# Third weight sums of the first two seven-product pairs ordered behind the operand's last low half, in a two-layer encoder trunk on one core

## The chip, the cores and the metric

The kernel runs on one core of one Trainium2 chip. The metric is the device time of one execution in microseconds (us), the median of several runs. A profiled execution gives the times of single instructions: PE is the matrix engine (TensorE), DVE is VectorE, ACT is ScalarE, POOL is GpSimd, and SP issues most transfers between the chip's main memory and its on-chip memory. Each engine works through a queue of its own in order; an instruction that waits holds up all that stand behind it on its engine, and nothing on the others unless they wait for it.

## The reference, cut to what matters

512 tokens of width 1024 go through two layers. In each, three token mixers (differential attention, a convolution module, neighbourhood attention) are merged by gates, projected and added to the residual stream; then come a gated feed-forward block of width 2816 and a gated input embedding:

```python
for i in range(DEPTH):                       # 2 layers
    ...
    merged = (ga * (ya @ w_br_a[i]) + gb * (yb @ w_br_b[i])
              + gc * (yc @ w_br_c[i]))
    x = x + merged @ w_o[i]
    h = rmsnorm(x, norm_ffn[i])
    x = x + (jax.nn.silu(h @ w_ffn_gate[i]) * (h @ w_ffn_up[i])) @ w_ffn_down[i]
    ...
```

The part that the change touches runs from the end of the merge, through `merged @ w_o` and the norm behind it, to the first blocks of the feed-forward products.

## The kernel before, in words

**Number format.** Matrix products are made in three passes. Every float32 operand is split into a high half (ScalarE, `act`, L143) and a low half (VectorE, the source minus the high half, `tt`, L157); `split` (L162) issues both. PE multiplies high by high, high by low and low by high (L177 to L179 in `mm3`, L983 to L985 in `seven`). So each weight and each activation that PE uses has been through ScalarE and then VectorE.

**The stages around the change.** `merge_b` (L767) ends the merge: its eight results are split into tiles that the profile calls mergeb_y and mergeb_v. `w_o` (L886) multiplies them by the output weights in eight groups of 24 matmuls (wo_mm), adds the residual (wo_x) and makes the operand for the next block (wo_h). The first two groups form a pair: PE does seven of eight chunks of each, and the last chunk of both at the end, so the last mergeb_v is needed there. The sum of squares goes through the norm (`norm`, L206): PE transposes it (L213), VectorE reduces it (L215) and scales it (L218), POOL takes the power (L222), PE transposes the result (L226).

**The feed-forward block** (`ffn`, L1039) runs over 22 blocks fb of 128 columns, in three parts of 8, 7 and 7. Block 0 multiplies gate and up weights by the operand in the plain way. Every other block is one pair of a gate and an up product in `seven` (L940), which replaces eight half-size products by seven. These need sums of weights and sums of the operand:

- The operand's sums are made by `quarters` (L911), once per pair of chunks. For j = 0 to 2 it is called from `w_o`, after chunks 2, 4 and 6, and for j = 3 from `ffn`, right ahead of block 0's products. Each call makes t1 to t4 on VectorE and splits them; for j = 2 and 3 the halves lie in wo_z tiles.
- The weights' sums are s1 = gate left + up left and s2 = up right + up left (both by a transfer that adds on arrival: SP loads at L950 and L951, POOL issues the accumulating transfers at L955), the third sum s3 = s1 + a22, and s4 = s3 + the right half of the gate weights. s3 and s4 are VectorE additions (L157, output ffn_qk, input ffn_r or ffn_wr). s1|s2, the gate weights, a22 and s3|s4 are then split. a22 is loaded at L953 (ffn_r), the gate weights at L952 (ffn_wr). The halves of s3|s4 are the tiles ffn_pt (odd fb) and ffn_y (even fb).

PE takes the products of a block in the order a11, a22, s2, a12, s1, s3, s4, so s3|s4 is wanted last.

**What sets the order.** PE's order is the order of the program text. The other engines are ordered by a scheduler that goes by priorities and by when inputs are estimated to be there; `seven` issues its loads and sums under a raised priority (L944), so they can stand far ahead of the stage they belong to. Where that is not wanted, `behind(i, then)` (L1020) gives instruction i a pure order behind `then`, without a semaphore. `seven` has three such orders. s3 stands behind the low half of a22 (L970). Where its argument `first` is true, for the first two blocks of the second and of the third part, s3 also stands behind `self.held` (L972), the low half that finished the block before. And the gating of the block before is ordered behind a copy (L1014).

Buffers: s3 and s4 have one buffer for all blocks; a22 has two (fb = 1, 2, then 3 takes that of 1); gate weights share three with all other weights.

Of the kernel before, what the change touches and what calls it, by code (L numbers as in the profile page):

```python
# [61 lines left out]
class Net:  # L62
# [848 lines left out]
    def quarters(self, x, h, j):  # L911


        one, two = slice(0, 256), slice(256, 512)
        g = lambda k: self.par(self.i, "ffn", k)
        f = []
        for k in (2 * j, 2 * j + 1):
            v = self.sb("t", [P, 512])
            self.act(v, x[k], AF.Copy, scale=g(k))
            f.append(v)  # L920
        b11, b12, b21, b22 = f[0][:, one], f[0][:, two], f[1][:, one], f[1][:, two]
        u = self.sb("t", [P, 2, 256])
        w = self.sb("t", [P, 2, 256])
        t1, t2, t3, t4 = u[:, 0], u[:, 1], w[:, 0], w[:, 1]
        self.tt(t1, b11, b12, ALU.subtract)
        self.tt(t2, b22, t1, ALU.add)
        self.tt(t3, b22, b12, ALU.subtract)
        self.tt(t4, t2, b21, ALU.subtract)
        if j < 2:
            d = [self.sb("rp" if n < 2 else "e", [P, 2, 256], F32R) for n in range(4)]  # L930
        else:
            d = [q for n in range(2) for q in self.zs[2 * j - 4 + n]]
        for o, t in zip(d, (t1, t2, t3, t4)):
            self.split(o[:, 0], o[:, 1], t)
        ha, hb = self.halves(h[2 * j]), self.halves(h[2 * j + 1])
        cut = lambda p, c: (p[0][:, c], p[1][:, c])
        return dict(b11=cut(ha, one), b21=cut(hb, one), b22=cut(hb, two),
                    **{f"t{n + 1}": (o[:, 0], o[:, 1]) for n, o in enumerate(d)})

    def seven(self, wg, wu, bs, tags, spare, md, first):  # L940


        nc = self.nc
        with self.tc.high_priority(offset=min(self.w_ahead, self.tc.cur_priority - self.p0)):  # L944
            lo, up = slice(0, 512), slice(512, 1024)
            g, a22 = self.sb("wr", [P, 1024]), self.sb("r", [P, 512])
            sums = self.sums[self.sevens % 3], self.sums[3]
            self.sevens += 1
            s1, s2, s3, s4 = (s[:, q:q + 512] for s in sums for q in (0, 512))
            nc.sync.dma_start(s1, wg[:, lo])  # L950
            nc.sync.dma_start(s2, wu[:, up])  # L951
            nc.sync.dma_start(g, wg)  # L952
            nc.sync.dma_start(a22, wu[:, up])  # L953
            for q in (s1, s2):
                nc.gpsimd.dma_start(q, wu[:, lo], accum_op=ALU.add)  # L955
            ws = {}

            def halve(hi, lo, src, names):
                i = self.split(hi, lo, src)
                for q, name in enumerate(names):  # L960
                    c = slice(q * 512, q * 512 + 512)
                    ws[name] = (hi[:, c], lo[:, c])
                return i

            wide = lambda: (self.sb("wh", [P, 1024], F32R), self.sb("wl", [P, 1024], F32R))
            halve(*wide(), g, ("a11", "a12"))
            low = halve(self.sb("kh", [P, 512], F32R), self.sb("a", [P, 512], F32R), a22, ("a22",))
            halve(*wide(), sums[0], ("s1", "s2"))
            i = self.tt(s3, s1, a22, ALU.add)
            self.behind(i, low)  # L970
            if first:
                self.behind(i, self.held)  # L972
            self.tt(s4, s3, g[:, up], ALU.add)
            halve(*spare, sums[1], ("s3", "s4"))
        A, C, Q = (self.ps(t, (P, 2, 256)) for t in tags)

        def product(out, w, b, first):
            wh, wl = ws[w]
            mm = nc.tensor.matmul
            for k in range(4):  # L980
                c = slice(k * P, k * P + P)
                bh, bl = bs[k][b]
                mm(out, wh[:, c], bh, start=first and k == 0, stop=False, skip_group_check=True)  # L983
                mm(out, wh[:, c], bl, start=False, stop=False, skip_group_check=True)  # L984
                mm(out, wl[:, c], bh, start=False, stop=k == 3, skip_group_check=True)  # L985
            self.chunk2()

        o = self.sb("t", [P, 2, 256])
        p1, p4 = o[:, 0], o[:, 1]
        p5 = self.sb("a", [P, 256])  # L990
        gg, uu = self.sb("t", [P, 2, 256]), self.sb("t", [P, 2, 256])
        product(A[:, 0], "a11", "b11", True)
        self.act(p1, A[:, 0], AF.Copy)
        product(Q[:, 0], "a22", "t4", True)
        self.act(p4, Q[:, 0], AF.Copy)
        product(C[:, 0], "s2", "t1", True)
        self.flush(self.act(p5, C[:, 0], AF.Copy))
        product(A[:, 0], "a12", "b21", False)
        product(Q[:, 0], "s1", "t3", False)
        product(A[:, 1], "s3", "t2", True)  # L1000
        product(C[:, 0], "s4", "b22", False)
        rb = self.rb.rearrange("p (a b) -> p a b", a=2)
        self.tt(p5, p4, p5, ALU.subtract)
        self.tt(gg[:, 0], A[:, 0], rb[:, 0], ALU.mult)
        self.tt(p1, A[:, 1], p1, ALU.subtract)
        self.tt(uu[:, 0], p1, Q[:, 0], ALU.subtract)
        self.tt(uu[:, 1], uu[:, 0], p5, ALU.add)
        self.tt(gg[:, 1], C[:, 0], p1, ALU.subtract)
        self.tt(gg[:, 1], gg[:, 1], rb[:, 1], ALU.mult)

        def rest(then):
            i = self.act(gg, gg, AF.Silu, table="silu")
            if then is not None:
                self.behind(i, then)  # L1014
            self.tt(gg, gg, uu, ALU.mult)
            self.held = self.split(md[:, 0, :], md[:, 1, :], gg.rearrange("p a b -> p (a b)"))

        self.pending.append(rest)
# [20 lines left out]
    def ffn(self, h, x):  # L1039
# [3 lines left out]
        st, hn, bs = [], [], self.four  # L1043
        spare = [[self.sb(t, [P, 1024], F32R) for _ in range(2)] for t in ("y", "pt")]
        md8 = [self.sb(t, [P, 2, 512], F32R) for t in ["v"] * 4 + ["z"] + ["y"] * 3]
        self.sums, self.sevens = [t for _ in range(2) for t in self.parts_of("qk", [1024], 2)], 0
        for part in PARTS:
            mids = []
            for f, fb in enumerate(part):
                tags = (("mm", "mm", "mm"), ("sc", "sc", "av"))[fb % 2]  # L1050
                md = md8[f]
                mids.append(md)
                wg, wu = self.a["w_fg"][i, fb], self.a["w_fu"][i, fb]
                if fb:
                    self.seven(wg, wu, bs, tags, spare[fb % 2], md, part[0] and f < 2)
                    continue
                g = self.sb("t", [P, 512])
                pg, pu = (self.ps(t) for t in tags[:2])
                for j in range(len(QUARTERS), 4):
                    self.four.append(self.quarters(x, h, j))  # L1060
                self.pair((pg, pu), (wg, wu), [h[k] for k in ORDER])

                def gate(pg=pg, g=g):
                    self.tt(g, pg, self.rb, ALU.mult)
                    self.act(g, g, AF.Silu, table="silu")

                self.ready(gate)

                def up(pu=pu, g=g, md=md):
                    self.tt(g, g, pu, ALU.mult)  # L1070
                    self.split(md[:, 0, :], md[:, 1, :], g)

                self.ready(up)
            self.flush()
            down = [self.a["w_fd"][i, m][:, part[0] * P:(part[-1] + 1) * P] for m in range(KD)]
            two = [self.ps(("mm", "sc")[fb % 2 == 0]) for _ in range(2)]
            self.pair(two, down[:2], mids)
            for m in range(KD):
                if m < 2:
                    ps = two[m]  # L1080
                else:
                    ps = self.ps("mm")
                    self.gemm(ps, down[m], mids)
                d = self.sb("t", [P, 512])
                self.tt(d, ps, self.rb, ALU.mult)
                self.tt(x[m], x[m], d, ALU.add)
                if part is PARTS[-1]:
                    if m in (0, 2):
                        qk = self.parts_of("qk", [2, 512], 2, F32R)
                    hn.append(self.norm_chunk(m, x[m], self.par(i, "ple", m),  # L1090
                                              qk[m % 2] if m < 4 else "z", st))
# [315 lines left out]
```

## Time and profile before

| what | value |
|---|---|
| median of three runs | 1793.07 us (1792.29 to 1793.09) |
| the profiled execution's own time | 1792.81 us |
| its span, from first to last instruction | 1791.0 us |
| PE, DVE, ACT busy in the span | 99%, 79%, 50% |
| mean granted clock of TensorE | 0.998 |

The page of the profile has the busy time of each engine, the chain of work that ended last, and groups of instructions. The timeline of an engine gives for each instruction its start and duration in us, its line, output and inputs, and in brackets how long the engine was idle ahead of it and what released it. Starts of neighbouring instructions can be closer than their durations, since instructions of one engine overlap a little. The granted clock (PEclk) is the share of full speed that TensorE's throttle allowed.

### The profile page before, as it was taken

To read this page: it belongs to the slowest core of one execution; us is meant where nothing else is said; L and a number is where in the kernel's file an instruction comes from. 1 tells how busy PE (TensorE), PEld (TensorE's weight loads), DVE (VectorE), ACT (ScalarE), POOL (GpSimd) and SP (SyncE) were. 2 spreads that over 40 slices of the span, in tenths; PEclk is the share of its full clock that TensorE was granted. 3 is DMA by queue.
4 is the path that set the end of the run, shared out by engine and by line. 5 is a ranking of instruction groups with operands and counts; after the bars stand their busy time and mean duration, and the time that the engine had idled before them with its cause. 6 is when DMAs were issued, how large, how long until landed. Compare 5 with 4: busy or idle time off the path is not lost.

```text
span 1791.0 us, 27255 instructions
## 1 busy us (share of the span) xinstructions
PE 1774.5 (99%) x10138; PEld 1559.7 (87%) x10138; DVE 1410.6 (79%) x2394; ACT 891.6 (50%) x1551; POOL 99.3 (6%) x142
## 2 busy tenths in 40 slices
PE   9999999999999999999999999999999999999998
PEld 7888888888799899998888888888887998989987
DVE  7877888997788587787776788889887885877776
ACT  5577555325565254454535765552355652534444
POOL 0000000000111011100000000000001110101000
PEclk9999999999999999999999999999999999999999
DMA  5665541334747365544447655422356563746332
GB/s 206 190 182 169 159 124 46 108 98 150 217 130 188 111 166 154 140 123 127 145 125 200 170 161 148 112 71 95 97 182 186 153 173 108 182 133 159 98 103 94
DMA packets 112212, 254.48 MB, mean 142 GB/s; under 512 B 14416, under 2 KB 19024, under 8 KB 112080
## 3 DMA queue, kind: packets, MB, share of 16 engines
q1 hardware_dynamic: 99264, 229.40, 41.9%
q0 software_dynamic: 12096, 22.03, 7.8%
q8 instruction: 80, 1.31, 0.3%
q10 hardware_dynamic: 720, 1.31, 0.2%
q14 instruction: 52, 0.43, 0.1%
HBM read 213.89 MB, written 7.34 MB: 124 GB/s over the span
## 4 chain that ended last, share of the span: by engine, by line
PE 91%; DVE 4%; DMA 2%; ACT 2%; issue 1%; SPq 0%; DVEq 0%; POOLq 0%; ACTq 0%
PE ffn_mm L177 5%; PE ffn_mm L178 5%; PE ffn_mm L179 5%; PE ffn_mm L985 4%; PE ffn_mm L984 4%; PE ffn_mm L983 4%; PE ffn_sc L985 3%; PE ffn_sc L984 3%; PE ffn_sc L983 3%; PE mergea_mm L178 2%; PE mergea_mm L179 2%; PE mergea_mm L177 2%; PE diff_sc L784 2%; PE gatec_mm L177 2%; PE gatec_mm L178 2%; PE gatec_mm L179 2%
## 5 line engine op out<-in xcount | busy, mean ns | idle before, releaser
L160 DVE SCALAR_TENSOR_TENSOR conv_z<-glu_z,pre_par,conv_z 128x512 f32<-128x512 f32 x240 | 179.6, 748 | 3.3
L143 ACT ACTIVATE ffn_wh<-ffn_wr 128x1024 fp32r<-128x1024 f32 (+1 forms) x94 | 94.9, 1015 | 110.0 <-PE ffn_mm L178 75.1
L157 DVE TENSOR_TENSOR ffn_wl<-ffn_wr,ffn_wh 128x1024 fp32r<-128x1024 f32 (+1 forms) x94 | 109.9, 1174 | 5.1 <-ACT ffn_wh L143 4.6
L955 POOL DMA_DIRECT2D ffn_qk<-w_fu x84 | 74.6, 996 | 550.5 <-DMA ffn_qk<-w_fu 218.1
L157 DVE TENSOR_TENSOR ffn_t<-ffn_mm,wo_rb 128x512 f32<-128x512 f32 (+1 forms) x66 | 40.0, 607 | 68.3 <-PE ffn_mm L179 68.3
L143 ACT ACTIVATE mergea_wh<-mergea_wr 128x1024 fp32r<-128x1024 f32 (+1 forms) x32 | 27.1, 846 | 96.8 <-PE mergea_mm L178 79.5
L177 PE MATMUL ffn_mm<-ffn_v,ffn_wh 128*128 128x512 f32 x176 | 68.5, 389 | 0.0
L178 PE MATMUL ffn_mm<-ffn_v,ffn_wh 128*128 128x512 f32 x176 | 68.5, 389 | 0.0
L179 PE MATMUL ffn_mm<-ffn_v,ffn_wl 128*128 128x512 f32 x176 | 68.5, 389 | 0.0
L157 DVE TENSOR_TENSOR ffn_wl<-ffn_qk,ffn_wh 128x1024 fp32r<-128x1024 f32 x42 | 51.4, 1225 | 19.9 <-ACT ffn_wh L143 19.9
L143 ACT ACTIVATE ffn_wh<-ffn_qk 128x1024 fp32r<-128x1024 f32 x42 | 44.5, 1060 | 43.7 <-PE ffn_mm L178 24.5
L157 DVE TENSOR_TENSOR ffn_t<-ffn_t,ffn_t 128x512 f32<-128x512 f32 (+1 forms) x48 | 31.4, 659 | 32.1 <-ACT ffn_t L143 31.5
L143 ACT ACTIVATE diff_a<-diff_sc,diff_s 128x512 f32<-128x512 f32 x32 | 22.0, 687 | 59.0 <-DVE diff_s L875 59.0
L983 PE MATMUL ffn_sc<-wo_h,ffn_wh 128*128 128x256 f32 x176 | 50.0, 284 | 0.0
L985 PE MATMUL ffn_sc<-wo_h,ffn_wl 128*128 128x256 f32 x176 | 49.8, 283 | 0.0
L984 PE MATMUL ffn_sc<-wo_h,ffn_wh 128*128 128x256 f32 x176 | 49.8, 283 | 0.0
L143 ACT ACTIVATE natten_wh<-natten_wr 128x1024 fp32r<-128x1024 f32 x24 | 25.4, 1058 | 41.4 <-issue 15.2
L984 PE MATMUL ffn_mm<-wo_h,ffn_wh 128*128 128x256 f32 x160 | 45.3, 283 | 0.0
L985 PE MATMUL ffn_mm<-wo_h,ffn_wl 128*128 128x256 f32 x160 | 45.3, 283 | 0.0
L983 PE MATMUL ffn_mm<-wo_h,ffn_wh 128*128 128x256 f32 x160 | 45.3, 283 | 0.0
L875 DVE TENSOR_REDUCE diff_s<-diff_sc 128x1 f32<-128x512 f32 x64 | 42.0, 684 | 3.5 <-PE diff_sc L784 3.4
L143 ACT ACTIVATE ffn_kh<-ffn_r 128x512 fp32r<-128x512 f32 x42 | 26.6, 632 | 32.8 <-PE ffn_mm L984 16.2
(825 smaller groups left out, 6577.0 us busy)
## 6 DMA issues: line engine op xcount, KB each, us to landing
ffn_wr<-w_fg SPq DMA_DIRECT2D x44, 512.0 KB, 3.9
ffn_qk<-w_fu POOLq DMA_DIRECT2D x84, 256.0 KB, 5.5
ffn_wr<-w_fd SPq DMA_DIRECT2D x32, 448.0 KB, 3.8
ffn_r<-w_fu SPq DMA_DIRECT2D x42, 256.0 KB, 4.8
ffn_qk<-w_fg SPq DMA_DIRECT2D x42, 256.0 KB, 3.9
ffn_qk<-w_fu SPq DMA_DIRECT2D x42, 256.0 KB, 4.2
natten_wr<-w_in SPq DMA_DIRECT2D x16, 512.0 KB, 4.1
natten_b<-bias SPq DMA_DIRECT2D x32, 256.0 KB, 3.8
```

Source lines behind the costliest of these rows:

```text
L143: i = self.nc.scalar.activation(out, in_, func, **kw)
L157: return self.nc.vector.tensor_tensor(out, a, b, op)
L160: return self.nc.vector.scalar_tensor_tensor(out, a, s, b, op0, op1)
L177: mm(out, wh, ah, start=first, stop=False)
L178: mm(out, wh, al, start=False, stop=False)
L179: mm(out, wl, ah, start=False, stop=last)
L784: self.nc.tensor.matmul(out, st4[:, u, qs], st[:, ks], start=n == 0, stop=n == 1)
L875: nc.vector.tensor_reduce(out=m[:, u:u + 1], in_=sc, op=ALU.max, axis=AX.X, negate=True)
L955: nc.gpsimd.dma_start(q, wu[:, lo], accum_op=ALU.add)
L983: mm(out, wh[:, c], bh, start=first and k == 0, stop=False, skip_group_check=True)
L984: mm(out, wh[:, c], bl, start=False, stop=False, skip_group_check=True)
L985: mm(out, wl[:, c], bh, start=False, stop=k == 3, skip_group_check=True)
```

## The change

`quarters` now keeps the last low half that it makes in `self.held`, and `seven` is told its block. For blocks 1 and 2, in each layer, s3 is ordered behind `self.held` as well. At that point `self.held` is the low half of t4 for j = 3: `quarters` is called for j = 3 ahead of block 0's products, and no block has yet set `self.held` anew when blocks 1 and 2 issue their sums. For the blocks that had the order already, nothing changes. The instructions and their operands stay the same; their places in the queues of VectorE, ScalarE and SP can change.

```diff
         for o, t in zip(d, (t1, t2, t3, t4)):
-            self.split(o[:, 0], o[:, 1], t)
+            self.held = self.split(o[:, 0], o[:, 1], t)
...
-    def seven(self, wg, wu, bs, tags, spare, md, first):
+    def seven(self, wg, wu, bs, tags, spare, md, first, fb):
...
             i = self.tt(s3, s1, a22, ALU.add)
             self.behind(i, low)
-            if first:
+            if first or fb < 3:
                 self.behind(i, self.held)
             self.tt(s4, s3, g[:, up], ALU.add)
...
-                    self.seven(wg, wu, bs, tags, spare[fb % 2], md, part[0] and f < 2)
+                    self.seven(wg, wu, bs, tags, spare[fb % 2], md, part[0] and f < 2, fb)
```

In the order that the scheduler then builds, in each layer: on VectorE s3 of block 1 moves from between two merge instructions to behind the last wo_z, s4 and the low half of s3|s4 to behind the norm's first instructions, two other pairs of neighbours change places; on ScalarE the high half of s3|s4 moves to behind the last wo_z; on SP the load of a22 for block 3 moves from ahead of three residual reads to behind the gate weights of block 3. PE and POOL keep their order.

## The prediction

> **What bounds the kernel now.** I read four views in this order: the page's busy shares with its chain, the waits of PE, the timelines of PE and VectorE around the longest of those waits, and the table of windows with the granted clock. From the page, the busy shares and the chain by engine:
>
> ```profile
> PE 1774.5 (99%) x10138; PEld 1559.7 (87%) x10138; DVE 1410.6 (79%) x2394; ACT 891.6 (50%) x1551; POOL 99.3 (6%) x142
> ...
> PE 91%; DVE 4%; DMA 2%; ACT 2%; issue 1%; SPq 0%; DVEq 0%; POOLq 0%; ACTq 0%
> ```
>
> PE is busy for 99% of the span and carries 91% of the chain that ended last. Work taken off any other engine is worth nothing by itself; only PE's idle or slowed time can be won. So the next view is the list of what PE waited for, the two longest entries (total, times, longest):
>
> ```profile
> PE wo_mm L178 <- DVE mergeb_v L157: 6.0, 2, 3.6
> PE pre_av L323 <- DVE pre_zeror L379: 1.1, 1, 1.1
> ```
>
> One wait stands out: 6.0 us in two pieces, one in each layer. In both, the output projection (wo_mm) waits for a low half that VectorE makes from the merged mixers (mergeb_v). All other entries are 1.1 us or less. PE's timeline at the first piece (start, duration, and in brackets the idle time before it and its releaser):
>
> ```profile
> 462.69 0.39 PE L177 MATMUL wo_mm<-mergeb_v,wo_wh 128*128 128x512 f32 x1
> ...
> 463.37 0.39 PE L177 MATMUL wo_mm<-mergeb_v,wo_wh 128*128 128x512 f32 x1
> 467.31 0.50 PE L178 MATMUL wo_mm<-mergeb_v,wo_wh 128*128 128x512 f32 x1 [3.56 <-DVE mergeb_v L157]
> ...
> 469.26 0.39 PE L177 MATMUL wo_mm<-mergeb_y,wo_wh 128*128 128x512 f32 x1
> ```
>
> and at the second:
>
> ```profile
> 1350.15 0.39 PE L177 MATMUL wo_mm<-mergeb_v,wo_wh 128*128 128x512 f32 x1
> 1352.99 0.75 PE L178 MATMUL wo_mm<-mergeb_v,wo_wh 128*128 128x512 f32 x1 [2.46 <-DVE mergeb_v L157]
> ...
> 1356.74 0.39 PE L178 MATMUL wo_mm<-mergeb_y,wo_wh 128*128 128x512 f32 x1
> ```
>
> The idle time is not the whole loss, so I count slips: how much later a matmul starts than it would at the undisturbed pace. The pace is three matmuls in 463.37 - 462.69 = 0.68 us, 0.227 us each. The matmul at 469.26 is the ninth after the one at 463.37; undisturbed it would start at 463.37 + 9 x 0.227 = 465.41. The first slip is 3.85 us. The matmul at 1356.74 is the tenth after 1350.15; undisturbed 1350.15 + 10 x 0.227 = 1352.42. The second slip is 4.32 us, although its wait was the shorter one. The table of windows says why (time, PE's busy time and count, then the other engines, PEclk, DMA share, GB/s):
>
> ```profile
> 467.30:469.30 2.00, 1.99 (x9) 1.65 (x10) 1.21 (x2) 1.40 (x2) 0.88 (x1) 1.00 0.88 182
> ...
> 1353.00:1356.50 3.50, 3.50 (x8) 2.76 (x9) 1.70 (x3) 2.44 (x3) 1.73 (x2) 0.51 1.09 233
> ```
>
> After the second wait the granted clock was 0.51 for 3.5 us, and eight matmuls took the time of some fifteen; after the first it was 1.00. What held VectorE in both places is seen in its own timeline, layer one and then layer two:
>
> ```profile
> 456.99 0.69 DVE L157 TENSOR_TENSOR gatec_x<-gatec_x,gateb_v 128x512 f32<-128x512 f32 x1
> 465.96 0.69 DVE L157 TENSOR_TENSOR ffn_qk<-ffn_qk,ffn_r 128x512 f32<-128x512 f32 x1 [8.29 <-DMA ffn_qk<-w_fu]
> 466.57 0.69 DVE L157 TENSOR_TENSOR mergeb_v<-gatec_x,mergeb_v 128x512 fp32r<-128x512 f32 x1
> ```
>
> ```profile
> 1351.64 0.69 DVE L157 TENSOR_TENSOR ffn_qk<-ffn_qk,ffn_r 128x512 f32<-128x512 f32 x1 [7.18 <-DMA ffn_qk<-w_fu]
> 1352.25 0.69 DVE L157 TENSOR_TENSOR mergeb_v<-gatec_x,mergeb_v 128x512 fp32r<-128x512 f32 x1
> ```
>
> The instruction that waits is s3 = s1 + a22 of fb = 1 (output ffn_qk), far ahead of its stage: it waits 8.29 and 7.18 us for the accumulating transfer into s1. The last low half of the merged operand stands right behind it in VectorE's queue, and PE waits for that one.
>
> **The change, part by part.** In each layer the added order puts s3 of fb = 1 behind the last low half of quarters (j = 3). s4, which adds to s3, the high half of s3|s4 on ScalarE and its low half on VectorE go with it. Nothing is added or removed in the arithmetic.
>
> (1) The wait in front of mergeb_v goes. What is late there next? VectorE is free when gatec_x ends, at 456.99 + 0.69 = 457.68, and its other input is the high half on ScalarE:
>
> ```profile
> 457.71 0.63 ACT L143 ACTIVATE mergeb_v<-gatec_x 128x512 fp32r<-128x512 f32 x1 [1.70 <-DVE gatec_x L157]
> ```
>
> It ends at 458.34, so the low half ends near 459.1. PE wants it one pace after 463.37, at 463.60: 4.5 us of margin. Both slips go whole: 3.85 + 4.32 = **8.17 us**.
>
> (2) What is moved costs VectorE 0.60 us for s3 (465.96 to the next start at 466.57), and in its old place for s4 and the low half, and ScalarE for the high half:
>
> ```profile
> 490.77 0.69 DVE L157 TENSOR_TENSOR ffn_qk<-ffn_qk,ffn_wr 128x512 f32<-128x512 f32 x1
> ...
> 492.85 1.22 DVE L157 TENSOR_TENSOR ffn_pt<-ffn_qk,ffn_pt 128x1024 fp32r<-128x1024 f32 x1
> ```
>
> ```profile
> 491.49 1.06 ACT L143 ACTIVATE ffn_pt<-ffn_qk 128x1024 fp32r<-128x1024 f32 x1
> ```
>
> That is 0.69 + 1.22 us of VectorE and 1.06 us of ScalarE that leave the stretch around 491 and land where VectorE and its neighbours look like this (VectorE; then POOL; then PE):
>
> ```profile
> 507.08 1.09 DVE L157 TENSOR_TENSOR wo_z<-ffn_t,wo_z 128x256 fp32r<-128x256 f32 x3
> 508.09 0.69 DVE L215 TENSOR_REDUCE wo_sm<-wo_tr 128x4 f32<-128x512 f32 x1
> 508.88 0.17 DVE L218 TENSOR_SCALAR wo_sm<-wo_sm 128x4 f32<-128x4 f32 x1
> 512.98 1.22 DVE L157 TENSOR_TENSOR ffn_wl<-ffn_qk,ffn_wh 128x1024 fp32r<-128x1024 f32 x1 [3.93 <-ACT ffn_wh L143]
> ```
>
> ```profile
> 509.13 1.03 POOL L222 TENSOR_TENSOR wo_rc<-wo_sm,pre_power 128x4 f32<-128x4 f32 x1 [38.93 <-DVE wo_sm L218]
> ```
>
> ```profile
> 512.59 0.60 PE L226 MATMUL wo_tr<-pre_ident,wo_rc 128*128 128x128 f32 x4
> 520.22 0.28 PE L983 MATMUL ffn_sc<-wo_rp,ffn_pt 128*128 128x256 f32 x1
> ```
>
> In the built order s3 stands behind the last wo_z and ahead of the reduction, s4 between the reduction and L218, the low half behind L218. So the chain reduction, L218, POOL, L226 gets 0.60 for s3 and as much for s4, 1.20 us, in front of it. POOL ends at 509.13 + 1.03 = 510.16, PE wants the column at 512.59: 2.43 us of margin, 1.23 left. The rest fits VectorE's hole of 3.93 us; the low half is needed by PE at 520.22, some 8 us after its new end. Cost 0; if the cover were gone, it could cost at most the 1.20 us per layer. From below it could even gain: VectorE loses up to 0.69 + 1.22 us of work ahead of the last wo_z and may get there earlier. But that is no time on PE; 0.
>
> (3) VectorE itself must follow PE. Up to the last wo_z it is nearly full:
>
> ```profile
> 495.00:508.00 13.00, 13.00 (x61) 10.78 (x60) 12.55 (x26) 10.73 (x20) 0.00 (x0) 1.00 0.33 110
> ```
>
> Its chain hangs on the ends of PE's wo_mm groups, which come earlier by the slip, and up to 1.91 us of work leave it. I take it to move with PE; that it stays where it is, is a rival below.
>
> (4) The transfer of a22 for fb = 3 needs the buffer that s3 reads. On SP it stood ahead of three reads of the residual; the built order puts it behind those and seven weight loads. The rows are its old issue, and ScalarE's high half of that a22:
>
> ```profile
> 466.68 0.33 SPq L953 DMA_DIRECT2D ffn_r<-w_fu  x1
> ```
>
> ```profile
> 526.06 0.63 ACT L143 ACTIVATE ffn_kh<-ffn_r 128x512 fp32r<-128x512 f32 x1 [0.94 <-PE ffn_mm L984]
> ```
>
> SP now stands behind it until s3 has read, about 508.09 + 0.60 = 508.7 on the old clock, and the transfer still has 17 us. Behind it on SP waits only the gate weight of fb = 4 and what follows, wanted later still. POOL's queue keeps its order: its accumulating transfers do not read s3. 0, with nothing at either end while the 17 us hold. The residual reads go out earlier, and only get margin.
>
> (5) For fb = 2 the added order changes nothing. Its s3 already stands behind the last wo_z:
>
> ```profile
> 518.29 0.69 DVE L157 TENSOR_TENSOR ffn_qk<-ffn_qk,ffn_r 128x512 f32<-128x512 f32 x1
> ```
>
> The sum: 8.17 us less, against the profiled execution 1792.81 - 8.17 = 1784.64 us. That execution lies 0.26 us below the median of the runs, so I forecast **1784.9 us** for the median.
>
> The unsure part of the sum is the clock. Beyond idle time the first slip has 3.85 - 3.56 = 0.29 us, the second 4.32 - 2.46 = 1.86 us, 1.57 more. If in the timed runs neither wait were followed by a slow stretch, the gain is 8.17 - 1.57 = 6.60; if both were, 9.74. I take the profiled row, since the three runs agree within 0.80 us, less than one such stretch.
>
> The Trainium skill, "TensorE: Matmul & The Clock Gate", Part 1, says that the clock halves after an idle window of about 3.4 us of a free-running counter. Here the row differs: the wait of 2.46 us was followed by 0.51, that of 3.56 us by 1.00. By that rule the slow stretch would not come from the second wait, and might not go with it; the sum would then be an estimated 6.6 us instead of 8.2.
>
> **The rivals.**
> - *The slow stretch stays.* The 0.51 has another cause, or comes in other runs differently. For it: the longer wait had none. Against: it begins at the very matmul that ends the wait. Gain 6.60, 1786.5 us; with both stretches in the runs before, 9.74, 1783.3 us.
> - *VectorE does not follow PE.* If the last wo_z stays at its absolute time, L226 stands 3.85 us earlier, and with 1.20 added against 2.43 of margin PE waits 2.62 us; in layer two, by the same margin, 4.32 + 1.20 - 2.43 = 3.09. Given back 5.71, gain 2.46: 1790.6 us. For it: the 12.55 of 13.00 us. Against: the moved work leaves exactly this stretch.
> - *The wait moves along with s3* (slower). s3 would wait at its new place as long as now, in front of the norm's reduction, and L226 would be late by 1.20 + 8.29 - 2.43 = 7.06 and 1.20 + 7.18 - 2.43 = 5.95 us: 13.01 - 8.17 = 4.84 us slower, 1797.9 us. It costs from a wait of 1.23 us on, and is slower than before from 1.23 + 8.17 / 2 = 5.3 us per layer. Against: s1 has landed by 465.96, some 38 us ahead of the new place.
> - *Nothing changes*: the low half of mergeb_v meets another wait as long. Then 1793.1 us. Against: part 1's 4.5 us of margin.
>
> **How the numbers follow.** Forecast 0.80, slow stretch 0.08, VectorE not following 0.05, wait moved 0.04, nothing 0.03. The range takes in the bounds of the clock, 1783.3 to 1786.5, with half the spread of the runs (0.40) below and the whole of it above, for a small part given back: 1782.9 to 1787.3 us; that holds the first two cases, and leaves the other 0.12 out. A difference of 0.2% (3.6 us) is about what a measurement of this kernel can tell from no change. Faster by more: 0.80 + 0.08 = 0.88. Within: 0.05 + 0.03 = 0.08. Slower: 0.04.
>
> **What would show it.** The waits of PE lose the entry on mergeb_v; the granted clock is 1.00 through the wo stage of both layers; s3 of fb = 1 appears behind the last wo_z without a wait; L226 has no idle time before it; ffn_wl behind the moved work starts as early, against PE, as now. If PE waits at L226, or for ffn_pt, the second rival holds in part; a slow stretch without a wait shows the first; s3 waiting for its transfer shows the third.

## The result, and the profile after

| | median, us | lowest to highest | runs |
|---|---|---|---|
| before | 1793.09 | 1792.29 to 1794.55 | 5 |
| after | 1784.92 | 1784.47 to 1785.96 | 5 |

The ratio after to before is 0.9953, with a 95% interval of 0.9939 to 0.9968: 8.2 us less. The profiled execution of after took 1785.96 us, its span is 1784.2 us.

The list of PE's waits in the profile after (engine and line, what it waited for, total us, times, longest):

```profile
PE natten_tr L709 <- ACT natten_e L143: 1.1, 2, 0.7
PE pre_av L323 <- DVE pre_zeror L379: 1.1, 1, 1.1
PE natten_tr L709 <- DVE natten_a L157: 0.9, 4, 0.3
PE diff_mm L588 <- ACT diff_rp L143: 0.6, 2, 0.3
PE natten_tr L709 <- DVE natten_pt L157: 0.6, 1, 0.6
```

The entry of 6.0 us on mergeb_v is gone, in both layers, and nothing of its size has come up. VectorE around the place that s3 has left (start, duration, line, output and inputs, idle time before it and its releaser):

```profile
457.58 0.68 DVE L157 TENSOR_TENSOR gatec_x<-gatec_x,gateb_v 128x512 f32<-128x512 f32 x1
458.97 0.69 DVE L157 TENSOR_TENSOR mergeb_v<-gatec_x,mergeb_v 128x512 fp32r<-128x512 f32 x1 [0.70 <-ACT mergeb_v L143]
464.84 1.37 DVE L157 TENSOR_TENSOR wo_x<-wo_x,wo_mm 128x512 f32<-128x512 f32 x2 [5.18 <-PE wo_mm L179]
```

The last low half of the merged operand now waits 0.70 us for its high half, and VectorE is then idle for 5.18 us until PE has finished: at this place VectorE waits for PE, no longer PE for VectorE. PE itself goes through the place at its pace, in the first layer:

```profile
463.96 0.39 PE L177 MATMUL wo_mm<-mergeb_v,wo_wh 128*128 128x512 f32 x1
464.18 0.39 PE L178 MATMUL wo_mm<-mergeb_v,wo_wh 128*128 128x512 f32 x1
```

The low half ended at 458.97 + 0.69 = 459.66, and PE read it at 464.18: 4.5 us of margin. Where s3 has gone to, on VectorE, then POOL, then PE:

```profile
503.40 1.09 DVE L157 TENSOR_TENSOR wo_z<-ffn_t,wo_z 128x256 fp32r<-128x256 f32 x3
504.40 0.69 DVE L157 TENSOR_TENSOR ffn_qk<-ffn_qk,ffn_r 128x512 f32<-128x512 f32 x1
505.01 0.69 DVE L215 TENSOR_REDUCE wo_sm<-wo_tr 128x4 f32<-128x512 f32 x1
505.61 0.69 DVE L157 TENSOR_TENSOR ffn_qk<-ffn_qk,ffn_wr 128x512 f32<-128x512 f32 x1
506.21 0.17 DVE L218 TENSOR_SCALAR wo_sm<-wo_sm 128x4 f32<-128x4 f32 x1
507.42 1.22 DVE L157 TENSOR_TENSOR ffn_pt<-ffn_qk,ffn_pt 128x1024 fp32r<-128x1024 f32 x1 [1.04 <-ACT ffn_pt L143]
```

```profile
506.46 1.03 POOL L222 TENSOR_TENSOR wo_rc<-wo_sm,pre_power 128x4 f32<-128x4 f32 x1 [35.73 <-DVE wo_sm L218]
```

```profile
509.33 0.60 PE L226 MATMUL wo_tr<-pre_ident,wo_rc 128*128 128x128 f32 x4
516.96 0.28 PE L983 MATMUL ffn_sc<-wo_rp,ffn_pt 128*128 128x256 f32 x1
```

s3 waits for nothing. POOL has the norm's column at 506.46 + 1.03 = 507.49, PE takes it at 509.33: 1.84 us of margin. The low half of s3|s4 ends at 508.64, 8.3 us before PE uses it. The granted clock in both wo stages is seen in this execution's table of windows (time, PE busy and count, the other engines, PEclk, DMA share, GB/s), the first layer's and the second's:

```profile
460.00:465.00 5.00, 5.00 (x24) 4.14 (x23) 0.16 (x1) 0.34 (x1) 1.02 (x2) 1.00 0.97 252
465.00:475.00 10.00, 10.00 (x46) 8.29 (x45) 9.22 (x14) 7.62 (x12) 2.65 (x3) 1.00 1.09 298
1345.00:1350.00 5.00, 5.00 (x24) 4.14 (x23) 1.45 (x3) 1.63 (x2) 1.01 (x2) 1.00 1.03 297
1350.00:1356.00 6.00, 6.00 (x28) 4.99 (x27) 5.22 (x7) 4.16 (x7) 2.62 (x3) 1.00 1.10 298
```

The spans of the two profiled executions differ by 6.8 us, not 8.2. Part of that is chance: of the five executions of after, the profiled one is the slowest, 1.04 us above the median, and its waits at natten_tr add up to 1.1 + 0.9 + 0.6 = 2.6 us, against 0.8 + 0.6 + 0.3 = 1.7 in the profile before, in a stage that the change does not touch.

### The profile page after: what moved, and what is told of

Same layout as the page of the kernel before. It is cut to its first block, busy times and chain, and to the rows that moved or that the text cites. A ratio compares the mean times of both kernels' runs of the same rounds, so it can differ in the third digit from the quotient of the medians.

```text
span 1784.2 us, 27269 instructions
## 1 busy us (share of the span) xinstructions
PE 1773.0 (99%) x10138; PEld 1559.2 (87%) x10138; DVE 1410.5 (79%) x2394; ACT 891.4 (50%) x1551; POOL 99.3 (6%) x142
## 4 chain that ended last, share of the span: by engine, by line
PE 92%; DVE 4%; ACT 2%; DMA 1%; issue 1%; SPq 0%; POOLq 0%; DVEq 0%; ACTq 0%
PE ffn_mm L178 5%; PE ffn_mm L177 5%; PE ffn_mm L179 5%; PE ffn_mm L985 4%; PE ffn_mm L984 4%; PE ffn_mm L983 4%; PE ffn_sc L985 3%; PE ffn_sc L984 3%; PE ffn_sc L983 3%; PE mergea_mm L178 2%; PE mergea_mm L177 2%; PE mergea_mm L179 2%; PE diff_sc L784 2%; PE gatec_mm L177 2%; PE gatec_mm L178 2%; PE gatec_mm L179 2%
```

## The experiments

**The theory.** The gain is PE's two slips behind mergeb_v, idle time and the half-clock stretch behind it; the new place costs nothing as long as the norm's column has margin. **The rivals.** The gain comes from other things that changed places (SP's order, or s4 and the halves of s3|s4, which left the wo stage); the slow stretch is no consequence of the wait; the new place already costs something.

Ratios below are to runs of the kernel before on the same chip. Medians of that kernel differ from one group of runs to the next (1793.1 to 1795.8), which is taken up under e7.

### One layer at a time

e1_layer_one:

```diff
-            if first or fb < 3:
+            if first or (fb < 3 and self.i == 0):
```

> The added order in the first layer alone. Theory (the gain is the two slips of PE behind mergeb_v): only the first slip goes, 3.85 us, so about 1789.2 us; PE keeps its wait of about 2.5 us at wo_mm in the second layer, with the granted clock near 0.5 behind it. Rival (the gain is in the other transfers and sums that change places, and counts once for the whole program): not half of 8.2 but nearly all or nearly none, 1785 or 1793 us.

Measured: 1790.26 us (1789.29 to 1790.99, 8 runs), ratio 0.9976 [0.9966, 0.9986]: 4.3 us less by the ratio, 4.5 by the medians (before: 1794.79). PE's waits and its timeline in the second layer:

```profile
PE wo_mm L178 <- DVE mergeb_v L157: 3.3, 1, 3.3
```

```profile
1346.25 0.39 PE L177 MATMUL wo_mm<-mergeb_v,wo_wh 128*128 128x512 f32 x1
1349.98 0.80 PE L178 MATMUL wo_mm<-mergeb_v,wo_wh 128*128 128x512 f32 x1 [3.34 <-DVE mergeb_v L157]
1350.57 0.63 PE L179 MATMUL wo_mm<-mergeb_v,wo_wl 128*128 128x512 f32 x1
...
1355.69 0.56 PE L179 MATMUL wo_mm<-mergeb_y,wo_wl 128*128 128x512 f32 x1
1356.09 0.40 PE L177 MATMUL wo_mm<-mergeb_y,wo_wh 128*128 128x512 f32 x1
```

The wait of the untouched layer has stayed, and the 14 matmuls behind it take some 0.43 us from start to start. The matmul at 1356.09 is the fifteenth after 1346.25; at 0.227 us each it would start at 1349.66. This slip is 6.43 us, of which 3.34 is the wait. In the execution that the prediction read, the same layer's slip was 4.32.

e2_layer_two:

```diff
-            if first or fb < 3:
+            if first or (fb < 3 and self.i == 1):
```

> The added order in the second layer alone. Theory: the second slip goes, 4.32 us where its wait is followed by the slow stretch, so about 1788.8 us; with the first layer's 3.85 it adds up to the whole. If the slow stretch has another cause and stays, the gain is 2.75 us, about 1790.3 us, and the granted clock still falls to about 0.5 near the start of wo in the second layer.

Measured: 1788.62 us (1788.55 to 1789.53, 5 runs), ratio 0.9967 [0.9955, 0.9980]: 5.9 us less by the ratio, 6.2 by the medians. The clock in the second layer's wo stage is 1.00, so the slow stretch went with the wait. In the first layer, where the wait stayed, there now is one:

```profile
PE wo_mm L178 <- DVE mergeb_v L157: 2.2, 1, 2.2
```

```profile
465.90:469.90 4.00, 4.00 (x11) 3.12 (x12) 2.59 (x4) 3.34 (x5) 1.75 (x2) 0.57 1.11 258
1340.00:1355.00 15.00, 15.00 (x67) 12.42 (x67) 9.12 (x13) 6.36 (x9) 3.57 (x4) 1.00 0.99 303
```

Each layer gives its own part: by the ratios 4.3 + 5.9 = 10.2 us, against 1794.8 x 0.0056 = 10.1 for both together (ratio 0.9944, e7 below). The first rival, in the form that the gain counts once, falls.

### Only past mergeb_v, and nothing else

e3_behind_merge: s3 of block 1 changes places with the last low half of the merged operand, and every other queue keeps the order of before (so the traces have it, in both layers):

```diff
-            self.split(mg[:, 0, :], mg[:, 1, :], acc[m])
+            self.merged = self.split(mg[:, 0, :], mg[:, 1, :], acc[m])
...
-            if first or fb < 3:
-                self.behind(i, self.held)
+            if first or fb == 1:
+                self.behind(i, self.held if first else self.merged)
```

> s3 of block 1 is ordered only behind the last low half of the merged operand: two instructions of VectorE change places in each layer, and nothing on ScalarE, POOL or SP. s3 then still waits for its transfer until about 466 us and holds the two residual additions by some 1.5 us. Theory: both waits of PE are gone, and the held additions are covered, so the whole gain, 8.2 us, about 1784.9 us. Rival (the gain comes from SP's residual reads going out earlier, or from taking s4 and the halves of s3 and s4 out of the wo stage): both stay as before, so no more than 2 us, above 1791 us.

Measured: 1784.75 us (1784.29 to 1785.92, 5 runs), ratio 0.9946 [0.9933, 0.9958]. VectorE:

```profile
458.22 0.69 DVE L157 TENSOR_TENSOR mergeb_v<-gatec_x,mergeb_v 128x512 fp32r<-128x512 f32 x1 [0.70 <-ACT mergeb_v L143]
464.35 0.69 DVE L157 TENSOR_TENSOR ffn_qk<-ffn_qk,ffn_r 128x512 f32<-128x512 f32 x1 [5.43 <-DMA ffn_qk<-w_fu]
464.96 1.28 DVE L157 TENSOR_TENSOR wo_x<-wo_x,wo_mm 128x512 f32<-128x512 f32 x2
```

s3 still waits 5.43 us for its transfer, but now in time in which VectorE would wait for PE anyway. This is the whole gain, from one exchange on one engine. The order on SP, and the move of s4 and the halves, contributed nothing that can be measured: this kernel and after differ by 0.2 to 0.4 us in the median, less than the spread of either.

### The other half of the change

e4_third_pair:

```diff
-            if first or fb < 3:
+            if first or fb == 2:
```

> The added order for block 2 alone; every queue has the order of the kernel before. Theory: that half of the change does nothing, 1793.1 us within the spread of the runs (0.8 us). Rival: if it were worth anything, below 1791 us.

Measured: 1794.08 us (1792.15 to 1796.38, 11 runs), ratio 0.9996 [0.9987, 1.0005]. Block 2's order does nothing; s3 of block 2 stood late enough already, and in the trace every queue has the order of before. The interval is also what such a comparison can tell here: 0.1%.

### How much the new place could bear

e5_hold4 and e5_hold10 put 4 and 10 passes over the last operand sum (its maximum with itself) ahead of s3 and of the norm's reduction. The reduction is ordered behind them, and two later low halves behind L218, so that the chain keeps its order:

```diff
             self.held = self.split(o[:, 0], o[:, 1], t)
+        for _ in range(10 if j == 3 else 0): self.held = self.tt(o[:, 1], o[:, 1].bitcast(F32), o[:, 1].bitcast(F32), ALU.max)
...
+        red = nc.vector.tensor_reduce(out=sm, in_=st, op=ALU.add, axis=AX.X)
+        ...  self.phase == "wo" and self.behind(red, self.held)
```

> The changed kernel with 4 extra VectorE passes of 0.34 us over the last operand sum (a maximum of it with itself), ahead of s3 and the norm's reduction: 1.34 us later. In the changed kernel the norm's column is ready 1.84 us before PE wants it. Theory (that margin is the price list of the new place): no cost, 1784.9 us, and no idle time ahead of L226. Rival (the new place already costs PE something, or VectorE's whole chain is at its limit): 1.3 us or more per layer, 1787.6 us or above.

Measured: 1785.07 us (1784.60 to 1785.50, 4 runs), ratio 0.9946 [0.9931, 0.9961]. A pass cost 0.43 us on average, not 0.34, so the delay was 1.73 us (505.24 - 503.51), and it met the margin nearly exactly:

```profile
503.51 1.81 DVE L157 TENSOR_TENSOR wo_z<-wo_z 128x256 fp32r<-128x256 f32 x4
505.24 0.68 DVE L157 TENSOR_TENSOR ffn_qk<-ffn_qk,ffn_r 128x512 f32<-128x512 f32 x1
```

```profile
507.29 1.03 POOL L222 TENSOR_TENSOR wo_rc<-wo_sm,pre_power 128x4 f32<-128x4 f32 x1 [35.91 <-DVE wo_sm L218]
```

```profile
508.37 0.65 PE L226 MATMUL wo_tr<-pre_ident,wo_rc 128*128 128x128 f32 x4
```

POOL ends at 508.32, PE takes the column at 508.37 without idle time. No cost: the new place was free, with 1.7 us to spare.

> The same with 10 passes, 3.35 us. Theory: L226 is late by 3.35 - 1.84 = 1.5 us in each layer, 3.0 us in all, 1787.9 us; if a slow stretch follows one of the waits, about 1.6 more. Rival (the norm's column isn't what sets PE there): no cost, 1784.9 us.

Measured: 1795.55 us (1794.65 to 1797.24, 10 runs), ratio 1.0005 [0.9996, 1.0015]: the whole gain is gone again. The rival that the norm's column does not matter there falls, but the size was far off. PE's waits, VectorE, POOL, and PE in the first layer:

```profile
PE wo_tr L226 <- POOL wo_rc L222: 7.1, 2, 3.6
```

```profile
503.48 4.56 DVE L157 TENSOR_TENSOR wo_z<-wo_z 128x256 fp32r<-128x256 f32 x10
507.96 0.69 DVE L157 TENSOR_TENSOR ffn_qk<-ffn_qk,ffn_r 128x512 f32<-128x512 f32 x1
...
509.76 0.16 DVE L218 TENSOR_SCALAR wo_sm<-wo_sm 128x4 f32<-128x4 f32 x1
509.83 1.22 DVE L157 TENSOR_TENSOR ffn_wl<-ffn_qk,ffn_wh 128x1024 fp32r<-128x1024 f32 x1
```

```profile
510.01 1.94 POOL L222 TENSOR_TENSOR wo_rc<-wo_sm,pre_power 128x4 f32<-128x4 f32 x1 [39.56 <-DVE wo_sm L218]
```

```profile
512.00 0.65 PE L226 MATMUL wo_tr<-pre_ident,wo_rc 128*128 128x128 f32 x4 [3.56 <-POOL wo_rc L222]
```

The passes took 4.48 us instead of 3.35, POOL's power 1.94 us instead of 1.03: 4.48 + 0.91 - 1.84 = 3.55, as measured, twice. From e5_hold4 to e5_hold10 it is 10.5 us: 7.1 are idle time, and the other 3.4 go with a stretch of 3.41 us at half clock behind each wait, 1.7 us each (granted clocks of 0.64 and 0.57 over the 4 us behind the two waits).

### The clock behind a wait

e6_late11, e6_late13 and e8_late8 make PE wait at the old place again, without a transfer: 11, 13 or 8 passes over the last merged chunk ahead of its split.

```diff
+            for _ in range(11 if m == KD - 1 else 0): self.tt(acc[m], acc[m], acc[m], ALU.max)
             self.split(mg[:, 0, :], mg[:, 1, :], acc[m])
```

> The changed kernel with 11 extra VectorE passes of 0.6 us over the last merged chunk (a maximum of it with itself) ahead of its split, in place of the wait for a transfer. The last low half then ends near 466.7 us on the first layer's clock, and PE waits about 2.5 us in each layer: 5 us for idle time, 1790 us, if no slow stretch follows. Theory (a wait of this length can be followed by 3.5 us at half clock, and it depends on when it falls, not on its length): one or both layers show a granted clock near 0.5, 1.6 us each, 1791 to 1793 us. Rival (the slow stretch of the second layer had nothing to do with the wait): the granted clock stays at 1.00, 1790 us.

Measured: 1795.47 us (1794.53 to 1798.02, 10 runs), ratio 1.0008 [0.9998, 1.0018]. PE waited 2.86 us for the high half and 0.23 and 0.22 us for the low half, and both layers had a slow stretch:

```profile
466.40:470.40 4.00, 3.73 (x11) 2.75 (x12) 2.94 (x4) 2.64 (x4) 1.76 (x2) 0.73 1.11 263
1354.50:1358.50 4.00, 3.78 (x10) 2.73 (x11) 2.48 (x4) 2.55 (x3) 1.72 (x3) 0.65 1.09 229
```

The rival without a connection falls: these waits are made by VectorE's passes, and the clock falls behind both. The time is 2.5 us above the top of what was expected. Some 1.2 of them are longer waits: a pass took 0.72 us, not 0.6, and PE waited 3.1 us per layer, not 2.5. The rest was not traced to a cause.

> The same with 13 passes: PE waits about 3.7 us in each layer, 7.4 us of idle time, 1792.3 us without a slow stretch, 1793.9 with one, 1795.5 with two. If the length of the wait decided (longer waits are followed by slow stretches, shorter ones are not), both layers would be slow here and neither with 11 passes. If the place in time decides, the two layers can differ.

Measured: 1798.82 us (1798.31 to 1800.46, 9 runs), ratio 1.0027 [1.0017, 1.0036]. PE waited 4.31 us in each layer, and both had a granted clock of 0.50 for the next 4 us. That alone does not tell length from place, since both layers were slow with 11 passes as well; the time is 3.3 us above the top again. The waits are longer than the 3.7 us expected, 1.2 us in all, and the clock stayed at 0.50 for 5.0 and 6.0 us behind them, where I had counted 3.5, which is some 2.3 us more.

> As with 11 extra passes ahead of the last merged split, but 8. The passes took 0.72 us each, so PE's wait should be 2.86 - 3 x 0.72 = 0.7 us per layer. If slow stretches follow only waits of some length, 0.7 + 0.4 us for the two pieces, twice: 2.2 us, 1787.1 us, granted clock 1.00. If any wait at this place brings one, about 1.6 us more per layer, 1790 us.

Measured: 1787.29 us (1786.84 to 1787.43, 4 runs), ratio 0.9955 [0.9942, 0.9969]; 2.2 us above after in its group of runs (e7), as expected without a slow stretch. PE waited 0.67 us and 0.22 us per layer, and no slow stretch followed:

```profile
464.00:468.00 4.00, 3.78 (x15) 2.91 (x16) 3.17 (x5) 2.70 (x4) 1.65 (x2) 1.00 1.10 261
1348.20:1352.20 4.00, 3.74 (x15) 2.89 (x16) 3.16 (x5) 2.65 (x4) 1.00 (x2) 1.00 1.12 241
```

### The pair of kernels once more

> The changed kernel itself once more, beside runs of the kernel before on the same chip. The runs of the kernel before spread from 1791.5 to 1796.9 us by now, those of the kernels without the wait by about 1.6. Theory (the slow stretches that follow the two waits differ from run to run and go with them): the changed kernel at 1784.9 us with a spread under 2 us, the kernel before at 1793 to 1796 us with a wider one, a gain between the idle bound of 6.6 and 9.7 us and nearer to the upper. Rival (the gain is a fixed 8.2 us): both spread alike.

Measured, the unchanged kernel after: 1785.14 us (1784.68 to 1785.72, 5 runs) against 1795.84 us (1793.22 to 1797.30, 9 runs), ratio 0.9944 [0.9931, 0.9958], 10.7 us. The spread is 1.0 us on one side and 4.1 on the other. Over all groups, the kernel before ran from 1791.51 to 1797.30 us, and the kernels without a wait at these places (after, e3, e5_hold4) from 1784.29 to 1785.96. So the uncertain part of the time lies in the kernel before, and goes with its waits. That the slow stretches, which differ from profile to profile, make up this spread fits every profile. Only one execution of each kernel has a trace, but the mean granted clock is on record for every run, to three decimals. Of the 51 runs of before in the experiments, 19 with 0.996 took 1796.0 us on average, 18 with 0.997 took 1794.4, 11 with 0.998 took 1793.4 and 3 with 0.999 took 1792.2; all 19 runs of the kernels without a wait had 0.999 or 1.000. One stretch of 3.41 us at half clock lowers such a mean by about 0.001.

## Why the prediction was right, step by step

- **What bounds the kernel, and the price of a wait on PE.** Right. PE's slips, not VectorE's idle time of 15.5 us, were the measure, and e1 and e2 show that each layer's slip can be had by itself.
- **Part 1, what is late next.** Right: 4.5 us of margin were forecast and measured. e3 shows that this exchange is the whole of the gain.
- **Part 2, the new place.** Right in the result, and shown by e5_hold4. Its margin was forecast at 1.23 us and is 1.84: part of the added 1.20 us was made up. From the last wo_z to L226 there are 5.51 us in before, 5.93 in after (509.33 - 503.40) and 5.46 in e3, where s4 and the halves stay at their old place: VectorE comes 0.42 us earlier against PE where that work has left. The other 0.19 is a gap between the reduction and L218 in before, which s4 now fills. ffn_wl behind the moved work starts 0.38 us after L226, 0.39 in before.
- **Part 3, VectorE follows PE.** Right. The last wo_z came from 507.08 to 503.40, 3.68 us earlier, although PE came to this stage 0.59 us later in this execution (463.96 against 463.37). The second rival's mechanism exists (e5_hold10 is its picture), but VectorE had 1.7 us left, and it did not set in.
- **Part 4, the a22 of block 3.** Right: its transfer went out at 505.12, and nothing waits for it. e3, where it goes out early, is no faster.
- **Part 5.** Right, by e4.
- **The sum.** The forecast of 8.17 us agrees with the first pair of medians to the second decimal; that is luck, since the same pair of kernels gave 10.7 in e7. The term that was mis-sized is the clock's. I priced it from one execution, where one of two waits was followed by a stretch of eight slow matmuls, and argued that three runs within 0.80 us left no room for more. Later runs show what was missed: the first layer's wait is followed by a slow stretch too in other profiles (e2: 0.57, e4: 0.63), and a stretch can be 14 matmuls long instead of eight (e1). In e7 the gain came out at 10.7 us, 1.0 above the 9.74 that I had taken for the upper end. The forecast time itself held, because it is the time of the kernel without the waits, and that hardly varies.
- **The rule on the clock.** The Trainium skill, "TensorE: Matmul & The Clock Gate", Part 1, speaks of an idle window of about 3.4 us of a free-running counter. The traces agree with the length and with the free run, but a window need not be idle as a whole: 1.87 of 3.41 us was enough. The length of the wait alone does not decide: waits of 2.18, 2.24, 2.46 and 2.86 us were followed by a slow stretch, one of 3.56 us in before was not, two of 3.56 us in e5_hold10 were. The borders of the stretches sort them. In e4 (PEclk is third from the right):

```profile
466.10:467.10 1.00, 1.00 (x4) 0.85 (x5) 0.25 (x1) 0.43 (x1) 0.00 (x0) 1.00 1.12 221
467.10:470.50 3.40, 3.40 (x9) 2.63 (x8) 3.16 (x4) 3.40 (x6) 1.76 (x2) 0.50 1.04 265
470.50:471.50 1.00, 1.00 (x6) 0.82 (x5) 1.00 (x3) 0.45 (x1) 0.00 (x0) 0.99 0.91 277
1353.50:1354.50 1.00, 0.24 (x1) 0.24 (x2) 0.71 (x2) 0.00 (x0) 0.81 (x2) 1.00 0.94 170
1354.60:1358.00 3.40, 3.40 (x9) 2.64 (x8) 2.13 (x3) 2.88 (x4) 1.41 (x2) 0.50 0.98 178
1358.00:1359.00 1.00, 1.00 (x6) 0.81 (x5) 1.00 (x2) 1.00 (x3) 0.00 (x0) 1.00 1.01 326
```

  Windows of 0.5 us put the two starts at 467.11 and 1354.57. They lie 887.46 us apart, 260 times 3.413. All eleven stretches behind these waits last 3.41 us or twice that, and where an execution has two, their starts lie 260 or 261 times 3.413 us apart. So in these traces the clock changes only at borders 3.41 us apart, which do not move with the waits. The 3.41 us ahead of a stretch held 1.87 to 3.41 us of waiting in all eleven cases. In before, counted back from the start at 1353.07, a border falls at 465.60 and cuts the first wait into 1.85 and 1.71 us: no stretch. A stretch lasted 6.83 us in just the three cases in which PE was still waiting when it began (e1, e6_late13 twice). This sorts all twelve cases; where between 1.85 and 1.87 us the limit lies is finer than the traces can tell, and no run shifted a wait against a border on purpose. The slow stretch did not stay without the wait: in after, e3, e5_hold4 and e7 the clock is 1.00 in both wo stages.

## What to carry to other kernels

Ask of every long wait who stands behind the waiting instruction in its queue, and whether the engine that bounds the kernel needs that one: VectorE's wait of 8.29 us cost PE 3.56 us only because one low half stood behind it, and exchanging the two gave everything. Work pulled far ahead by priorities is safe only behind the last instruction that the bounding engine wants soon. And price a wait on PE as idle time plus a possible stretch at half clock (here 3.41 or 6.83 us of it), from several executions, since the second part changes from run to run.

## What the runs showed of the hardware that I had not expected

- Waits on PE of 2.2 to 4.3 us were followed by a granted clock of 0.50 to 0.73 over the next 4 us in eleven of twelve cases here; a pair of waits of 0.67 and 0.22 us was not (two cases). The stretch itself is at 0.50, for 3.41 us in eight cases and 6.83 us in three.
- POOL's power over 128x4 took 1.03 us in after and 1.94 us in e5_hold10, where VectorE started a 128x1024 subtraction 0.18 us ahead of it. The Trainium skill, "SBUF — State Buffer", section "Who interferes with whom", says that a VectorE instruction with two on-chip inputs and a GpSimd instruction that reads the same memory exclude each other; by that rule POOL waits out VectorE's instruction, which ended at 511.05, 0.90 us before POOL's end at 511.95. The trace agrees, with no experiment of its own. Once per layer it is seen in after as well: the power at 313.36 took 1.50 us, and a VectorE instruction with two inputs, started 0.11 us ahead of it, ended 0.86 us before its end.
- A VectorE pass that reads what the pass before it wrote came 0.46 us after it at 128x256 (a row of 4 lasts 1.81 us and one of 10 4.56 us, a single pass 0.42), where passes that do not were 0.34 us apart.
